# A row maximum that skips NaNs: keys on two engines against in-place halves on three, with longer loads and results stored by groups

## The chip, the cores and the metric

The kernel runs on one core of a Trainium2 chip. The metric is device time in microseconds for one execution, so lower is better. The core has several engines that run side by side: VectorE (DVE), ScalarE (ACT), GpSimd (POOL) and SyncE (SP), which here issues the transfers; 16 DMA engines move the data between the device's memory and the on-chip buffers of 128 partitions.

## The reference

The input is 32 x 2048 rows of 2048 float32 numbers, 512 MB in all, of which one in ten is NaN. For each row the largest number that is not NaN is wanted.

```python
def setup_inputs():
    batch, seq, dim = 32, 2048, 2048
    x = np.random.randn(batch, seq, dim).astype(np.float32)
    mask = np.random.rand(batch, seq, dim) < 0.1
    x[mask] = np.nan
    return {"x": x, "axis": -1}

def reference(x: np.ndarray, axis: int) -> np.ndarray:
    return np.nanmax(x, axis=axis).astype(np.float32)
```

Both kernels work on the bit patterns: they map them such that a NaN never wins.

## The kernel before

The 65536 rows are cut into 128 blocks. In a block each of the 128 partitions holds four whole rows, which lie next to each other in memory: 32 KB per partition, 4 MB per block, and the whole block is one contiguous piece of the input. The loop over the blocks `m` has three steps:

- SP issues the load of block `m` into `xt` (line 51, `xt<-in_x_dram`). The pool `io` has three buffers, and a buffer is free again once ACT has read it.
- ACT reads the numbers as int32 and writes a float32 key `kt` (line 53): the square of the scaled distance of the bit pattern from a constant. For numbers of the size drawn here the largest has the smallest key, and NaN a larger one. The pool `keys` has two buffers of 32 KB.
- DVE takes the minimum of the keys of each row (line 60, `acc<-kt`), four results per partition and block.

Behind the loop the 512 results per partition are turned back into numbers at once: a square root on ACT (line 70, with a table load of its own), two Newton rounds on DVE (lines 73 to 79), a linear step on ACT (line 81) and a cast (line 89). Then 64 transposes of 32x32 on DVE (line 100) bring them into the order of the output, and a single store writes them (line 104). The tile framework places the waits between the engines; each engine works through its instructions in program order.

Of the kernel before, what the change touches and what calls it, by code (L numbers as in the profile page):

```python
# [1 line left out]

# [4 lines left out]


@with_exitstack  # L10
def kernel(
    ctx: ExitStack,
    tc: tile.TileContext,
    x: bass.AP,
    axis: bass.AP,
    out: bass.AP,
):
    nc = tc.nc
    P = nc.NUM_PARTITIONS
    f32 = mybir.dt.float32  # L20
    i32 = mybir.dt.int32

    nd = len(x.shape)
    assert axis in (-1, nd - 1), axis
    D = x.shape[-1]

    x_bits = x.bitcast(i32).flatten_outer_dims()
    R = x_bits.shape[0]
    C = 4
    assert R % (P * C) == 0  # L30
    M = R // (P * C)
    x_ck = x_bits.rearrange("(m p c) d -> m p c d", p=P, c=C)

    out_flat = out.flatten_outer_dims().rearrange("r c -> (r c)")
    out_pn = out_flat.rearrange("(q s) -> q s", q=P)

    CG = float(0x50000000)
    SCALE = 2.0**-31
    BIAS = -CG * SCALE

    io = ctx.enter_context(tc.tile_pool(name="io", bufs=3))
    keys = ctx.enter_context(tc.tile_pool(name="keys", bufs=2))
    sing = ctx.enter_context(tc.tile_pool(name="sing", bufs=1))

    bias_t = sing.tile([P, 1], f32)
    nc.vector.memset(bias_t, BIAS)  # L46
    acc = sing.tile([P, M, C], f32)

    for m in range(M):
        xt = io.tile([P, C, D], i32)  # L50
        nc.sync.dma_start(out=xt, in_=x_ck[m])  # L51
        kt = keys.tile([P, C, D], f32)
        nc.scalar.activation(  # L53
            out=kt,
            in_=xt,
            func=mybir.ActivationFunctionType.Square,
            bias=bias_t,
            scale=SCALE,
        )
        nc.vector.tensor_reduce(  # L60
            out=acc[:, m, :],
            in_=kt,
            axis=mybir.AxisListType.X,
            op=mybir.AluOpType.min,
        )

    NQ = M * C
    accf = acc.rearrange("p m c -> p (m c)")
    y = sing.tile([P, NQ], f32)
    nc.scalar.activation(y, accf, mybir.ActivationFunctionType.Sqrt)  # L70
    for it in range(2):
        r = sing.tile([P, NQ], f32, tag=f"nr{it}")
        nc.vector.reciprocal(r, y)  # L73
        t = sing.tile([P, NQ], f32, tag=f"nt{it}")
        nc.vector.tensor_mul(t, accf, r)  # L75
        s = sing.tile([P, NQ], f32, tag=f"ns{it}")
        nc.vector.tensor_add(s, t, y)  # L77
        y = sing.tile([P, NQ], f32, tag=f"ny{it}")
        nc.vector.tensor_scalar_mul(y, s, 0.5)  # L79
    gf = sing.tile([P, NQ], f32)  # L80
    nc.scalar.activation(  # L81
        gf,
        y,
        mybir.ActivationFunctionType.Copy,
        bias=CG,
        scale=-(2.0**31),
    )
    gb = sing.tile([P, NQ], i32)
    nc.vector.tensor_copy(out=gb, in_=gf)  # L89

    B = 32
    assert M % P == 0
    U = M // P
    fin = sing.tile([P, U, P, C], i32)
    g4 = gb.rearrange("p (q u c) -> p q u c", u=U, c=C)
    for u in range(U):
        for j in range(C):
            for bi in range(P // B):
                for bj in range(P // B):
                    nc.vector.transpose(  # L100
                        out=fin[bi * B : (bi + 1) * B, u, bj * B : (bj + 1) * B, j],
                        in_=g4[bj * B : (bj + 1) * B, bi * B : (bi + 1) * B, u, j],
                    )
    nc.sync.dma_start(
        out=out_pn, in_=fin.rearrange("q u p c -> q (u p c)").bitcast(f32)
    )


# [1 line left out]
_INS = ['x', 'axis']  # L110
_OUTS = [((32, 2048), 'float32')]
#: Inputs that are plain numbers.
_NUMBERS = {'axis': -1}


# [26 lines left out]
```

## Time and profile before

| what | value |
|---|---|
| median of 12 runs | 1297.43 us (1297.26 to 1297.86) |
| profiled execution | 1297.38 us, span 1295.6 us |
| DVE, ACT, POOL busy | 1138.4, 915.4, 0.2 us |
| loads | 128 of 4096 KB, median 21.9 us from issue to landing |
| data moved | 537.19 MB, mean 415 GB/s over the span |

The span runs from the first to the last instruction. In a group's row stand its line, engine, operation, output and input with their shapes, the count, then the busy time in microseconds and the mean duration in nanoseconds, and last the idle time of the engine just before these instructions with what ended it. A timeline row begins with start and length in microseconds.

### The profile page before, as it was taken

Reading aid. Unit: us, or ns where it says so; the run is one execution under the profiler, and the core shown is the slowest. Engines: PE = TensorE matmul, PEld = TensorE weight load, DVE = VectorE, ACT = ScalarE, POOL = GpSimd, SP = SyncE. Lnnn points to the kernel's source line nnn. Section 1 sums busy time; section 2 is a strip of 40 time slices with the busy share of each in tenths; the row PEclk is TensorE's granted clock in tenths of the full one; section 3 lists DMA queues with packets and bytes.
Section 4 is the critical chain, followed back from the end, with each engine's and each line's share of the span. In section 5 each row is a group of like instructions: output and inputs, shape, how many; then the busy total and the mean of one; then the engine's idle time right before and its main releaser. Section 6 shows DMA issues by size and latency. Waiting matters only on the chain.

```text
span 1295.6 us, 761 instructions
## 1 busy us (share of the span) xinstructions
DVE 1138.4 (88%) x202; ACT 915.4 (71%) x132; POOL 0.2 (0%) x4
## 2 busy tenths in 40 slices
DVE  3988988988998988998998998998898998998998
ACT  4776776776776776776776776776777777777760
POOL 0000000000000000000000000000000000000000
DMA  9999999999999999999999999999999999999940
GB/s 405 437 430 428 437 432 426 437 434 424 436 435 425 434 435 425 435 435 425 435 435 425 436 434 427 434 434 429 431 436 427 431 437 428 430 437 428 430 197 8
DMA packets 18582, 537.19 MB, mean 415 GB/s; under 512 B 2064, under 2 KB 2064, under 8 KB 2192
## 3 DMA queue, kind: packets, MB, share of 16 engines
q1 hardware_dynamic: 18576, 537.14, 96.4%
q14 instruction: 6, 0.05, 0.0%
HBM read 536.87 MB, written 0.26 MB: 415 GB/s over the span
## 4 chain that ended last, share of the span: by engine, by line
DMA 73%; ACT 24%; DVE 3%; issue 0%; ACTq 0%; SPq 0%; DVEq 0%
DMA xt<-in_x_dram 73%; ACT kt L53 24%; DVE fin L100 1%; DVE acc L60 1%; DVE r L73 1%; DVE s L77 0%; DVE t L75 0%; DVE y L79 0%; ACTq L53 0%; ACT gf L81 0%; ACT y L70 0%; DVE gb L89 0%; SPq L51 0%; DVEq L137 0%
## 5 line engine op out<-in xcount | busy, mean ns | idle before, releaser
L60 DVE TENSOR_REDUCE acc<-kt 128x4 f32<-128x8192 f32 x128 | 1111.7, 8686 | 151.0 <-ACT kt L53 151.0
L53 ACT ACTIVATE kt<-xt,bias_t 128x8192 f32<-128x8192 int32 x128 | 911.6, 7122 | 329.0 <-DMA xt<-in_x_dram 329.0
L100 DVE STREAM_TRANSPOSE fin<-gb 32x32 int32<-32x32 int32 x64 | 15.9, 248 | 0.9
L53 ACT ACT_TABLE_LOAD x1 | 1.3, 1283 | 13.0 <-DMA xt<-in_x_dram 13.0
L81 ACT ACTIVATE gf<-y 128x512 f32<-128x512 f32 x1 | 0.6, 629 | 10.6 <-DVE y L79 10.6
L73 DVE RECIPROCAL r<-y 128x512 f32<-128x512 f32 x2 | 6.7, 3353 | 0.7 <-ACT y L70 0.7
L70 ACT ACTIVATE y<-acc 128x512 f32<-128x512 f32 x1 | 0.6, 629 | 7.5 <-DVE acc L60 7.5
L75 DVE TENSOR_TENSOR t<-acc,r 128x512 f32<-128x512 f32 x2 | 1.4, 691 | 0.1
L77 DVE TENSOR_TENSOR s<-t,y 128x512 f32<-128x512 f32 x2 | 1.4, 691 | 0.1
L70 ACT ACT_TABLE_LOAD x1 | 1.3, 1283 | 0.0
L89 DVE CAST gb<-gf 128x512 int32<-128x512 f32 x1 | 0.4, 427 | 0.7 <-ACT gf L81 0.7
L79 DVE TENSOR_SCALAR y<-s 128x512 f32<-128x512 f32 x2 | 0.9, 426 | 0.1
L46 DVE MEMSET bias_t<- 128x1 f32 x1 | 0.1, 59 | 0.8 <-PEq L123 0.8
L123 POOL MEMSET const-bfloat16-1.0<- 128x1 bf16 x1 | 0.1, 102 | 0.0
L123 POOL MEMSET const-uint8-127<- 128x1 uint8 x1 | 0.1, 102 | 0.0
L123 POOL MEMSET const-float32-0.0<- 128x1 f32 x1 | 0.1, 99 | 0.2 <-issue 0.2
L123 POOL MEMSET const-float32-1.0<- 128x1 f32 x1 | 0.1, 99 | 0.0
## 6 DMA issues: line engine op xcount, KB each, us to landing
xt<-in_x_dram SPq DMA_DIRECT2D x128, 4096.0 KB, 21.9
out_dram<-fin SPq DMA_DIRECT2D x1, 256.0 KB, 2.0
```

The lines of the kernel that those rows point to most:

```text
L46: nc.vector.memset(bias_t, BIAS)
L53: nc.scalar.activation(out=kt, in_=xt, func=mybir.ActivationFunctionType.Square, bias=bias_t, scale=SCALE,)
L60: nc.vector.tensor_reduce(out=acc[:, m, :], in_=kt, axis=mybir.AxisListType.X, op=mybir.AluOpType.min,)
L70: nc.scalar.activation(y, accf, mybir.ActivationFunctionType.Sqrt)
L73: nc.vector.reciprocal(r, y)
L75: nc.vector.tensor_mul(t, accf, r)
L77: nc.vector.tensor_add(s, t, y)
L79: nc.vector.tensor_scalar_mul(y, s, 0.5)
L81: nc.scalar.activation(gf, y, mybir.ActivationFunctionType.Copy, bias=CG, scale=-(2.0**31),)
L89: nc.vector.tensor_copy(out=gb, in_=gf)
L100: nc.vector.transpose(out=fin[bi * B : (bi + 1) * B, u, bj * B : (bj + 1) * B, j], in_=g4[bj * B : (bj + 1) * B, bi * B : (bi + 1) * B, u, j],
L123: nc = _bacc.Bacc("TRN2", target_bir_lowering=False, num_devices=1)
```

## The change

The work is laid out anew.

- The input is read in 16 groups of rows (`GROUPS`: a list of groups, each a list of tiles, each a list of loads, each a list of pieces, counted in rows per partition). Twelve groups have five tiles of eight rows per partition, so 40 rows; the four last have one tile of eight rows each. In a group each partition holds rows that lie next to each other: the load of a full tile takes 64 KB per partition, and in the large groups the pieces of neighbouring partitions lie 320 KB apart. The tiles of the last three groups are loaded in smaller parts: 4+2+2 rows, 2+2+1+1+1+1 rows, and eight single rows.
- There is no key tile. ACT, POOL and DVE work in turn on the same `xt`, in pieces of 3, 3 and 2 rows. ACT (line 94) reads the upper 16 bits of each number as int16 (every second 16-bit element) and writes uint16 in place: a number's upper half h becomes 0x7F7F - h, and the NaN's, on the other slope of Prelu, becomes 32768. POOL (line 102) computes 0x7F7F minus that, in place, as int16: a number gets its old upper half back, a NaN becomes a large negative number. DVE (line 110) takes the maximum of each row over the whole float32 numbers.
- `io` still has three buffers, now of 64 KB per partition; a buffer is free once DVE has reduced its last piece.
- At the end of each group two small DVE instructions (lines 118 and 127) turn a row of nothing but NaNs into NaN, and the group's results are stored without a transpose. The store of a group is issued on SP behind a load of the second next group (line 91), the last two at the end (line 132).
- A one-element activation ahead of the loop (line 71) loads the activation table.

```diff
+FULL = [[3, 3, 2]]
+GROUPS = [[FULL] * 5] * 12 + [
+    [FULL],
+    [[[2, 2], [2], [2]]],
+    [[[2], [2], [1], [1], [1], [1]]],
+    [[[1], [1], [1], [1], [1], [1], [1], [1]]],
+]
...
     io = ctx.enter_context(tc.tile_pool(name="io", bufs=3))
-    keys = ctx.enter_context(tc.tile_pool(name="keys", bufs=2))
+    res = ctx.enter_context(tc.tile_pool(name="res", bufs=3))
...
-    for m in range(M):
-        xt = io.tile([P, C, D], i32)
-        nc.sync.dma_start(out=xt, in_=x_ck[m])
-        kt = keys.tile([P, C, D], f32)
-        nc.scalar.activation(
-            out=kt,
-            in_=xt,
-            func=mybir.ActivationFunctionType.Square,
-            bias=bias_t,
-            scale=SCALE,
-        )
-        nc.vector.tensor_reduce(
-            out=acc[:, m, :],
-            in_=kt,
-            axis=mybir.AxisListType.X,
-            op=mybir.AluOpType.min,
-        )
...
+    stores = []
+    r0 = 0
+    for s, g in zip(rows, GROUPS):
+        xg = xr[r0 : r0 + P * s].rearrange("(p s) d -> p (s d)", p=P)
+        og = of[r0 : r0 + P * s].rearrange("(p s) -> p s", p=P)
+        r0 += P * s
+        acc = res.tile([P, s], f32, tag="acc")
+        at = 0
+        for tl in g:
+            xt = io.tile([P, WIDE * D], i32, tag="xt")
+            base = at
+            for ld in tl:
+                c = sum(ld)
+                nc.sync.dma_start(
+                    out=xt[:, (at - base) * D : (at - base + c) * D],
+                    in_=xg[:, at * D : (at + c) * D],
+                )
+                if len(stores) > 1:
+                    nc.sync.dma_start(**stores.pop(0))
+                for c in ld:
+                    xp = xt[:, (at - base) * D : (at - base + c) * D]
+                    nc.scalar.activation(
+                        out=xp.bitcast(u16)[:, 1::2],
+                        in_=xp.bitcast(i16)[:, 1::2],
+                        func=PRELU,
+                        bias=top,
+                        scale=-1.0,
+                        alpha=float(TOP - LOW) / (EDGE - NAN),
+                    )
+                    nc.gpsimd.tensor_scalar(
+                        out=xp.bitcast(i16)[:, 1::2],
+                        in0=xp.bitcast(u16)[:, 1::2],
+                        scalar1=-1.0,
+                        scalar2=float(TOP),
+                        op0=ALU.mult,
+                        op1=ALU.add,
+                    )
+                    nc.vector.tensor_reduce(
+                        out=acc[:, at : at + c],
+                        in_=xp.bitcast(f32).rearrange("p (c d) -> p c d", c=c),
+                        axis=mybir.AxisListType.X,
+                        op=ALU.max,
+                    )
+                    at += c
+        none = res.tile([P, s], i32, tag="none")
+        nc.vector.tensor_scalar(
+            out=none,
+            in0=acc,
+            scalar1=NONE,
+            scalar2=float(0x00C00000),
+            op0=ALU.is_equal,
+            op1=ALU.mult,
+        )
+        fin = res.tile([P, s], i32, tag="fin")
+        nc.vector.tensor_tensor(
+            out=fin, in0=acc.bitcast(i32), in1=none, op=ALU.bitwise_or
+        )
+        stores.append(dict(out=og, in_=fin))
+    for st in stores:
+        nc.sync.dma_start(**st)
```

Everything behind the old loop (lines 67 to 106 of the kernel before: root, Newton rounds, casts, transposes, the single store) is removed.

## Prediction

> **What bounds the kernel now.** I read four views. First the shares by engine and the chain that ended last:
>
> ```profile
> DVE 1138.4 (88%) x202; ACT 915.4 (71%) x132; POOL 0.2 (0%) x4
> DMA 73%; ACT 24%; DVE 3%; issue 0%; ACTq 0%; SPq 0%; DVEq 0%
> ```
>
> No compute engine is full, and the chain is DMA with ACT links. A chain "DMA 21.9, ACT 7.1, DMA 21.9" could mean a loop that waits for buffers, so the second view is the busy time by stretches (columns: stretch, length, DVE, ACT, POOL busy, clock, DMA share, GB/s):
>
> ```profile
> 100.00:600.00 500.00, 446.80 (x52) 366.62 (x52) 0.00 (x0) 1.00 1.00 432
> 600.00:1200.00 600.00, 535.97 (x63) 438.97 (x63) 0.00 (x0) 1.00 1.00 432
> 1247.00:1296.00 49.00, 42.16 (x75) 9.66 (x4) 0.00 (x0) 1.00 0.02 6
> ```
>
> The DMA share is 1.00 for the whole streaming part: the rings never run dry, so the transfer rate is the bound and the ACT links of the chain are only buffers handed back in time. The last stretch has no loads: 49 us of pure tail. Third, the timeline gives the ends of the stream and the order of the tail:
>
> ```profile
> 12.99 1.28 ACT L53 ACT_TABLE_LOAD   x1 [12.99 <-DMA xt<-in_x_dram]
> 21.44 17.28 DVE L60 TENSOR_REDUCE acc<-kt 128x4 f32<-128x8192 f32 x2 [20.58 <-ACT kt L53]
> ...
> 1247.71 7.12 ACT L53 ACTIVATE kt<-xt,bias_t 128x8192 f32<-128x8192 int32 x1 [2.58 <-DMA xt<-in_x_dram]
> 1254.85 1.28 ACT L70 ACT_TABLE_LOAD   x1
> 1254.87 8.69 DVE L60 TENSOR_REDUCE acc<-kt 128x4 f32<-128x8192 f32 x1 [1.01 <-ACT kt L53]
> 1263.59 0.63 ACT L70 ACTIVATE y<-acc 128x512 f32<-128x512 f32 x1 [7.45 <-DVE acc L60]
> ...
> 1275.97 16.72 DVE L100 STREAM_TRANSPOSE fin<-gb 32x32 int32<-32x32 int32 x64
> 1292.72 0.35 SPq L104 DMA_DIRECT2D out_dram<-fin  x1
> ```
>
> The first 4 MB land at 12.99 and the last at about 1247.7: 127 loads in 1234.7, so 9.72 us per load, 2.43 us per row of each partition. After the last landing come ACT 7.1, DVE 8.7, then 12.4 of root and Newton steps and cast (1263.6 to 1276.0), 16.7 of transposes, and 2.9 from the last transpose to the span's end: 48 in all. Last, the groups give the prices:
>
> ```profile
> L60 DVE TENSOR_REDUCE acc<-kt 128x4 f32<-128x8192 f32 x128 | 1111.7, 8686 | 151.0 <-ACT kt L53 151.0
> L53 ACT ACTIVATE kt<-xt,bias_t 128x8192 f32<-128x8192 int32 x128 | 911.6, 7122 | 329.0 <-DMA xt<-in_x_dram 329.0
> L75 DVE TENSOR_TENSOR t<-acc,r 128x512 f32<-128x512 f32 x2 | 1.4, 691 | 0.1
> L70 ACT ACTIVATE y<-acc 128x512 f32<-128x512 f32 x1 | 0.6, 629 | 7.5 <-DVE acc L60 7.5
> ```
>
> Two sizes of one engine give fixed part and slope. ACT: (7122-629)/7680 = 0.845 ns an element, 196 ns fixed. DVE: (8686-691)/7680 = 1.041 ns; two back-to-back reduces take 17.28, so 8.64 each, 0.11 us fixed.
>
> **The change part by part.**
>
> *The removed tail.* The root, both Newton rounds, the casts, the 64 transposes and the second table load go: 1263.6 to 1292.7, 29.1 us, all on the end path. All of it is gained only if nothing later takes its place.
>
> *The loads.* 61 of 8 MB, then 8 rows as 4+2+2, 8 as 2+2+1+1+1+1, 8 single rows. Bytes are the same, so 128 x 9.72 remains the floor: landing of tile 60 (the last full one) at 12.99-9.72+61x19.44 = 1189.1, of the last row 58.3 later, 1247.4. Two unknowns. Half as many long transfers may save something: the profile's best slices move 437 GB/s against a mean of 432, so 0 to 14 us if the whole gap were per-load cost; 2 is my value, as the rate is nearly flat. And a partition's run now lies 320 KB from the next one (40 rows of 8 KB) where it lay 32 KB. Here a rule of the Trainium skill speaks against the change ("DMA: Bandwidth & Descriptors", "Latency and other measured facts"): for 16 KB pieces, a row pitch of 512 KB gave 207 GB/s where the padded layout gave 214, and wider powers of two much less. The row here is 432 at a 32 KB pitch. Taken whole, 3.4% of 1234 is 42 us more; by the row, nothing. 320 KB is not a power of two and the pieces are 64 KB, so I take nothing, and keep 42 as an end.
>
> *Stores.* One store at the end becomes 16, on the SP queue with the loads. Each of the twelve 20 KB ones goes behind a load of two groups later, when its result is long done, so SP doesn't wait there. The old store took 2.0 from issue to landing; what one takes from the loads' engines lies between 0 and 0.5; 0.2 x 12 = 2.4. In the taper SP does wait: the store of tile 59's group blocks the loads behind it until tile 59 is reduced, that of tile 60 likewise, that of tile 61 likewise. About 9 us of load gaps follow, which the DVE backlog below covers. Without that cover they would be in the end.
>
> *Buffers.* kt goes; three xt of 64 KB are freed by DVE, not ACT. Per piece of 3, 3, 2 rows: ACT 0.196+0.845n = 5.39, 5.39, 3.66, sum 14.4; DVE 0.11+1.041n = 6.51, 6.51, 4.37, sum 17.39; both under the 19.44 of the transfer. With POOL as below, DVE starts a tile 11.0 after its landing and ends it at 28.4. The DMA has 38.9 of queued loads at that moment, so 10 us of slack for the next load: no gap.
>
> *POOL.* Before, POOL does four one-element memsets (102 ns); no row bounds its rate per element. Two statements of the Trainium skill, "GPSIMD Engine Reference", disagree: "Elementwise — side-by-side cycle accounting" has 1.03 cycles for bodies of up to two operations but calls 1.8 the best case of a tight loop, and "Performance pitfalls for Q7 kernels" gives about 1.9 for reads with small steps; "Engine selection" calls one-input work roughly line-rate. At its 1.2 GHz that is an estimate of 0.86 ns or of 1.5 to 1.6 ns. Per tile, with 0.2 fixed per instruction (twice the memset): 14.7 us or 25.2 us, against 19.44. By the first, POOL is hidden; by the second it is the bound. I take 0.86: the instruction has one tensor input, two operations and a 4-byte step[...]. The ends stay 0.85 and 1.6. The built program puts one set-up instruction ahead of POOL's first piece and ACT's table load ahead of the loop (1.28 in the old row); the first 8 MB land at 22.7, and the first buffer may come back 10 us late, so both are free up to that.
>
> *Group ends.* Two small DVE instructions per group, 16 times. By the rows 59 ns (memset) to 248 ns (transpose), 0.1 each, and 12 of the groups end in steady state where DVE has 2.05 idle a tile. The unknown is a lock with POOL: the Trainium skill ("SBUF — State Buffer", "Who interferes with whom") says a DVE operation with two SBUF inputs, or in a two-port mode, waits for a POOL instruction under way, while a reduce never does. No row here has both. Price 0 to 9 us on the four last groups (one POOL piece of up to 3.7 each for three of them); I take 1. In steady state up to 10 per group is covered by DVE's idle time (5 x 2.05).
>
> *The new tail.* At 1189.1 the last full tile lands, and DVE is still on the tile before. It starts tile 60 at 1200.1 and then has 17.39, tile 61 as four pieces of two rows (4 x 4.37 = 17.48), tile 62 (2 x 4.37 + 4 x 2.24 = 17.70) and tile 63 (8 x 2.24 = 17.92): 70.5, without a pause, since a row arrives each 2.43 and takes DVE 2.2. The taper lets DVE make up only some 10% of its lag. The reduces end at 1270.6, although the last row has landed by about 1257 with SP's gaps and passed ACT and POOL by 1261 (1.93 + 1.96). The store's 2.9 follows: 1273.5. Plus stores 2.4, lock 1, small operations 0.6, less 2 for the longer loads: a span of 1275.5. The profiled execution took 1297.38 for a span of 1295.6, so 1.8 lies around it: 1277.3, and as that execution is within 0.05 of the median of the twelve runs, it needs no other correction: 1277, a gain of 20. Of the 29 removed, about 9 come back as DVE's backlog: 48 us after the last landing become about 27.
>
> **The rivals.**
>
> *POOL becomes the bound (slower).* It decides from 1.15 ns an element: (19.44-0.6)/16384. At 1.5 ns a tile takes 25.2, 64 take 1611, and with start and end some 1645; at 1.6 about 1740. For it: two of the four statements, and 16-bit halves converted on both sides. Against it: one input, two operations. Chance 0.17.
>
> *The wide pitch slows the loads.* 42 us more on the DMA: it ends at about 1290, DVE catches up a little more, and the time is 1315. At half that price it would be about 1297, no change. Chance 0.08, of it 0.03 no change and 0.01 faster.
>
> *DVE isn't late.* If the taper did what its shape suggests, the end would be 1247.4 + 1.93 + 1.96 + 2.24 + 2.9 = 1256.4, time 1258, a little more with SP's gaps. DVE's 11 us start lag and 2.2 of 2.43 speak against it; a faster load rate doesn't help DVE. Chance 0.05.
>
> That the change isn't what it says is out: the built program has 61 long loads, three pieces per tile on each of three engines, and stores where the code has them.
>
> **How the numbers follow.** A measurement of this kernel tells about 0.2% (2.6 us) from no change. The forecast has 0.70, own range 1263 to 1292 (longer loads helping by up to 14, the lock by 9, stores by 6). With POOL 0.17, pitch 0.08, DVE in time 0.05: faster 0.70+0.05+0.01 = 0.76, same 0.03, slower 0.17+0.04 = 0.21. The range leaves out POOL's case and the best of the others: 1259 to 1316.
>
> **What would show it.** Right: POOL's groups at about 5.5 us for 128x6144; DMA share 1.00 to about 1190; the chain's last 70 us in the reduces of DVE without idle; the last load landing 10 us or more before the last reduce starts. Wrong: POOL busy over 95% with DVE waiting for it and the DMA share near 0.75 (the POOL rival); GB/s below 425 with all engines waiting for loads (pitch); DVE waiting for POOL in the last 20 us (DVE in time); idle before the two small DVE operations of several us (lock).

## The result and the profile after

The changed kernel takes 1284.56 us (median; 1284.3 to 1284.92) against 1297.42 before: a ratio of 0.9901, 95% interval 0.9892 to 0.991, so 12.9 us or 1.0% faster. The profiled execution has a span of 1282.7. The forecast was 1277, range 1259 to 1316.

The page of the changed kernel: busy time by engine, the chain that ended last, and the groups (busy, mean ns, idle before).

```profile
DVE 1143.1 (89%) x234; ACT 1203.8 (94%) x203; POOL 1204.4 (94%) x205
DMA 42%; POOL 23%; DVE 18%; ACT 12%; issue 5%; ACTq 0%; DVEq 0%
L110 DVE TENSOR_REDUCE acc<-xt 128x3 f32<-128x6144 f32 (+2 forms) x201 | 1116.0, 5582 | 135.4 <-POOL xt L102 135.4
L118 DVE TENSOR_SCALAR none<-acc 128x40 int32<-128x40 f32 (+1 forms) x16 | 24.7, 1543 | 0.4
```

ACT rose from 71% to 94% and POOL from nothing to 94%: two engines that the forecast had at three quarters are almost full. And sixteen small DVE operations (L118) take 1.5 us each on average instead of 0.1. The same groups with the shapes kept apart give the prices for the pieces:

```profile
L94 ACT ACTIVATE xt<-xt,top 128x6144 uint16<-128x6144 int16 x122 | 858.6, 7111 | 58.1 <-DMA xt<-in_x_dram 58.1
L102 POOL TENSOR_SCALAR xt<-xt 128x6144 int16<-128x6144 uint16 x122 | 856.7, 7022 | 60.5 <-ACT xt L94 55.7
L94 ACT ACTIVATE xt<-xt,top 128x2048 uint16<-128x2048 int16 x12 | 30.0, 2569 | 8.9 <-DMA xt<-in_x_dram 8.9
L102 POOL TENSOR_SCALAR xt<-xt 128x2048 int16<-128x2048 uint16 x12 | 29.6, 2465 | 3.8 <-ACT xt L94 2.9
```

From two sizes: ACT (7111-2569)/4096 = 1.109 ns an element, POOL (7022-2465)/4096 = 1.113. The loads still set the steady part (columns of the stretches as before):

```profile
100.00:600.00 500.00, 456.51 (x89) 483.90 (x78) 483.93 (x79) 1.00 1.00 432
600.00:1180.00 580.00, 530.63 (x102) 561.54 (x90) 562.73 (x90) 1.00 1.00 434
1180.00:1240.00 60.00, 58.27 (x15) 55.27 (x13) 58.74 (x12) 1.00 0.67 277
1240.00:1283.00 43.00, 40.16 (x20) 26.71 (x11) 30.53 (x13) 1.00 0.56 227
```

The DMA share is 1.00 up to 1180 and then falls to 0.67 and 0.56, while DVE is busy 98 of the last 103 us. The timeline shows this end (start, length, engine):

```profile
1185.86 46.81 ACT L94 ACTIVATE xt<-xt,top 128x6144 uint16<-128x6144 int16 x9 [0.65 <-DMA xt<-in_x_dram]
...
1200.24 6.55 DVE L110 TENSOR_REDUCE acc<-xt 128x3 f32<-128x6144 f32 x1
...
1222.33 4.09 DVE L118 TENSOR_SCALAR none<-acc 128x8 int32<-128x8 f32 x1
1226.27 4.41 DVE L110 TENSOR_REDUCE acc<-xt 128x2 f32<-128x4096 f32 x1
1230.60 0.62 DVE L127 TENSOR_TENSOR fin<-acc,none 128x8 int32<-128x8 int32 x1
...
1244.13 1.96 DVE L118 TENSOR_SCALAR none<-acc 128x8 int32<-128x8 f32 x1
...
1256.54 14.99 ACT L94 ACTIVATE xt<-xt,top 128x2048 uint16<-128x2048 int16 x6 [4.82 <-DMA xt<-in_x_dram]
...
1262.02 2.18 DVE L118 TENSOR_SCALAR none<-acc 128x8 int32<-128x8 f32 x1
...
1266.59 13.24 DVE L110 TENSOR_REDUCE acc<-xt 128x1 f32<-128x2048 f32 x6
1279.86 0.17 DVE L118 TENSOR_SCALAR none<-acc 128x8 int32<-128x8 f32 x1
```

Tile 60 has landed at 1185.86. DVE begins it at 1200.24 and then runs to 1279.86 with 0.4 us of idle time. In that run stand the three small pairs of groups 12 to 14 (counted from 0; a pair is L118 and L127): 4.09+0.62, 1.96+0.86 and 2.18+0.42, 10.1 us in all. The last pair, when POOL is done, takes 0.17+0.17.

### The profile page after: what moved, and what is told of

It reads as the page before. It is cut to its first block, busy times and chain, and to the rows that moved or that the text cites. A ratio compares the mean times of both kernels' runs of the same rounds, so it can differ in the third digit from the quotient of the medians.

```text
span 1282.7 us, 1065 instructions
## 1 busy us (share of the span) xinstructions
DVE 1143.1 (89%) x234; ACT 1203.8 (94%) x203; POOL 1204.4 (94%) x205
## 4 chain that ended last, share of the span: by engine, by line
DMA 42%; POOL 23%; DVE 18%; ACT 12%; issue 5%; ACTq 0%; DVEq 0%
DMA xt<-in_x_dram 42%; POOL xt L102 23%; DVE acc L110 18%; ACT xt L94 12%; DVE none L118 1%; DVE fin L127 0%; ACTq L94 0%; DVEq L110 0%; DVEq L127 0%
## 5 line engine op out<-in xcount | busy, mean ns | idle before, releaser
L102 POOL TENSOR_SCALAR xt<-xt 128x6144 int16<-128x6144 uint16 (+2 forms) x201 | 1204.2, 5991 | 69.7 <-ACT xt L94 58.6
L94 ACT ACTIVATE xt<-xt,top 128x6144 uint16<-128x6144 int16 (+2 forms) x201 | 1202.3, 6084 | 67.0 <-DMA xt<-in_x_dram 67.0
L110 DVE TENSOR_REDUCE acc<-xt 128x3 f32<-128x6144 f32 (+2 forms) x201 | 1116.0, 5582 | 135.4 <-POOL xt L102 135.4
L118 DVE TENSOR_SCALAR none<-acc 128x40 int32<-128x40 f32 (+1 forms) x16 | 24.7, 1543 | 0.4
L127 DVE TENSOR_TENSOR fin<-acc,none 128x40 int32<-128x40 int32 (+1 forms) x16 | 4.5, 280 | 0.4
```

What stands on the lines that cost most here:

```text
L94: nc.scalar.activation(out=xp.bitcast(u16)[:, 1::2], in_=xp.bitcast(i16)[:, 1::2], func=PRELU, bias=top, scale=-1.0, alpha=float(TOP - LOW ...
L102: nc.gpsimd.tensor_scalar(out=xp.bitcast(i16)[:, 1::2], in0=xp.bitcast(u16)[:, 1::2], scalar1=-1.0, scalar2=float(TOP), op0=ALU.mult, op1= ...
L110: nc.vector.tensor_reduce(out=acc[:, at : at + c], in_=xp.bitcast(f32).rearrange("p (c d) -> p c d", c=c), axis=mybir.AxisListType.X, op=A ...
L118: nc.vector.tensor_scalar(out=none, in0=acc, scalar1=NONE, scalar2=float(0x00C00000), op0=ALU.is_equal, op1=ALU.mult,)
L127: nc.vector.tensor_tensor(out=fin, in0=acc.bitcast(i32), in1=none, op=ALU.bitwise_or)
```

## The experiments

Two things had to be told apart: what the small pairs and the loads that SP holds back are worth at the end, and why ACT and POOL take 1.11 ns an element. The first theory was that the end is DVE's backlog (the work that lies before it and keeps it busy without a pause), in which the pairs wait for POOL ("lock"). The rival was that SP, waiting 65 us in all ahead of three stores, brings the last loads too late.

**Stores at the end.** The stores of the last five groups come behind all loads, and `res` gets six buffers instead of three to hold their results; nothing else changes.

```diff
-    res = ctx.enter_context(tc.tile_pool(name="res", bufs=3))
+    res = ctx.enter_context(tc.tile_pool(name="res", bufs=6))
...
-                if len(stores) > 1:
+                if len(stores) > 1 and gi < 13:
```

> The small DVE operations stay where they are; only the stores of the last five groups are issued after all loads, so that SP isn't held ahead of the late loads. Theory 'lock' with DVE's backlog as the end: the loads land some 10 us sooner and ACT and GpSimd finish sooner, but DVE has no idle time to give back: within 1.5 us of the changed kernel's 1284.56. It may move by the few us that a lock gets longer or shorter, since GpSimd's pieces then lie differently. Theory 'held loads': 9 to 10 us faster, 1275.

Measured: 1284.33 (1284.14 to 1284.55), 0.99 of before (0.9887 to 0.9913). The timeline has ACT and the last reduces:

```profile
1185.91 75.76 ACT L94 ACTIVATE xt<-xt,top 128x6144 uint16<-128x6144 int16 x21 [0.66 <-DMA xt<-in_x_dram]
...
1266.33 13.24 DVE L110 TENSOR_REDUCE acc<-xt 128x1 f32<-128x2048 f32 x6
```

ACT now works without a pause to 1261.7, so the loads are no longer late, and yet DVE's last reduces begin at 1266.33, where they began at 1266.59. The held loads cost nothing in the changed kernel; the rival is out.

**Small pairs deferred.** The last four groups share one result tile, and one pair over 32 columns comes behind all reduces (`finish` issues a pair and notes its stores); the stores of the last five groups are late, as above.

```diff
...
+        if gi < 12:
+            finish(acc, s, [og])
+        else:
+            touts.append(og)
...
+    finish(tacc, 32, touts)
```

> The two small DVE operations of the last four groups are moved behind all reduces (one pair over 32 columns instead of four pairs), and the stores of these groups and of the group before them go to the end, so that SP never waits ahead of a load. Theory 'lock': in the changed kernel these pairs took 10.1 us of DVE's time in its unbroken run from 1200.2 to 1280.2 because they wait for GpSimd instructions under way; taken away, DVE ends about 9 us sooner, less about 1 for four stores in a row: 1284.56 - 8 = 1276 to 1277. Theory 'held loads' (SP waits of 65 us ahead of the late loads set the end): also faster, by the about 10 us that ACT waited for the last two sets of loads (4.1 + 4.8), 1275; so this run alone doesn't tell them apart, stores_end does. If both are wrong: no change.

Measured: 1280.24 (0.9869, 0.9856 to 0.9882): 4.3 faster than the changed kernel, where 8 were expected. The direction holds, half of the gain doesn't. The timeline of this run says where most of it went:

```profile
1186.14 75.91 ACT L117 ACTIVATE xt<-xt,top 128x6144 uint16<-128x6144 int16 x21 [0.55 <-DMA xt<-in_x_dram]
1193.35 78.68 POOL L125 TENSOR_SCALAR xt<-xt 128x6144 int16<-128x6144 uint16 x21 [0.36 <-ACT xt L117]
1269.52 2.29 DVE L133 TENSOR_REDUCE tacc<-xt 128x1 f32<-128x2048 f32 x1 [0.25 <-POOL xt L125]
1272.06 2.29 DVE L133 TENSOR_REDUCE tacc<-xt 128x1 f32<-128x2048 f32 x1 [0.25 <-POOL xt L125]
```

DVE now waits 0.25 for POOL before each row, and ACT and POOL have 21 pieces without a pause. Behind DVE's backlog stood that of POOL: DVE's reduces end at 1274.34, only 5.5 earlier than in the changed kernel (1279.83). Of these, 1.4 are lost behind them, where four stores wait for the one pair, not one (from the last reduce to the end of the span 4.3 us, before 2.9). Note also the distance of the last two rows, 2.54 us: in pieces of one row POOL is slower than the loads (2.43 a row), so the finest part of the taper adds to its lag.

**The intermediate in PSUM.** One edit to the changed kernel takes away what the pair needs from the buffer's ports, with nothing moved (PSUM is a second on-chip memory, beside the buffer that holds the tiles):

```diff
+    ps = ctx.enter_context(
+        tc.tile_pool(name="ps", bufs=2, space=bass.MemoryType.PSUM)
+    )
...
-        none = res.tile([P, s], i32, tag="none")
+        none = ps.tile([P, s], i32, tag="none")
```

> The changed kernel with the intermediate of the small pair in PSUM instead of the on-chip buffer, nothing moved. Theory 'lock needs both sides in the buffer': the first of the pair falls from 1.4 (12 groups) and 2.7 (three tail groups) to about 0.2, the second, now with one input from the buffer, to 0.2; DVE's backlog is 9 shorter, and ACT and GpSimd become the end as in defer_small, with SP's held loads on top: 1280 to 1283. Rival 'any small DVE operation waits for GpSimd': the rows stay at 1 to 4 us and the time at 1284.5.

Measured: 1278.43 (0.9855, 0.9838 to 0.9871), 6.1 faster than the changed kernel and 1.6 below the range expected. The groups of the changed kernel (L118, L127) and of this run (L121, L130):

```profile
L118 DVE TENSOR_SCALAR none<-acc 128x8 int32<-128x8 f32 x4 | 8.4, 2100 | 0.0
L127 DVE TENSOR_TENSOR fin<-acc,none 128x8 int32<-128x8 int32 x4 | 2.1, 519 | 0.0
...
L121 DVE TENSOR_SCALAR none<-acc 128x40 int32<-128x40 f32 x12 | 2.4, 203 | 0.4
L121 DVE TENSOR_SCALAR none<-acc 128x8 int32<-128x8 f32 x4 | 0.6, 161 | 0.0
L130 DVE TENSOR_TENSOR fin<-acc,none 128x8 int32<-128x8 int32 x4 | 0.6, 154 | 0.0
```

The first of the pair fell from 2100 ns (8 columns) to 161, the second from 519 to 154. That is the lock shown: the same operation on the same data, beside the same POOL work, waits with its output in the buffer and doesn't with its output in PSUM. It is the rule that the forecast named (the Trainium skill, "SBUF — State Buffer", "Who interferes with whom"): an operation in a two-port mode, or with two inputs from the buffer, waits for POOL's instruction under way. The second of the pair has two such inputs; that the first is in a two-port mode is not shown by itself. The size is what it could not say: up to 4.1 us a time, with POOL pieces of 2.5 to 4.7. Here too DVE waits 0.25 for POOL before each of the last rows, and its reduces end at 1273.72; with one store behind the last pair instead of four, the span is 2.0 shorter than in the run before.

**Forms by themselves.** Two tiles of 2 MB, one instruction at a time, executed once.

> Not the task's computation: two 2 MB tiles, on which ACT, GpSimd and DVE run the changed kernel's instructions one at a time over 4096 elements, in forms that differ in the step of input and output and in the type; then twelve GpSimd instructions in a row beside which DVE runs reduces and the small pair, once with the intermediate in the on-chip buffer and once in PSUM. In the changed kernel ACT took 4845 ns and GpSimd 4746 for 4096 elements (1.11 ns an element), ACT in the kernel before 0.845 an element, so 3660. Theory 'step': writing (or reading) 16-bit values at a step of 4 bytes costs a third more, alone too: 4.8 us for the stepped form, 3.7 for the contiguous one, and the two mixed forms tell reading from writing. Theory 'contention': ACT and GpSimd slow each other in the kernel; alone the stepped form takes 3.7. Theory 'type': all 16-bit forms take 4.8. Lock: with GpSimd busy the small DVE operation with an output in the buffer takes 1 to 4 us, the reduces their usual 4.4; if a lock needs both sides in the buffer, the PSUM versions take about 0.2.

The timeline (lines 87 and 89 to 92 are ACT: stepped to stepped in place; stepped to contiguous; contiguous to stepped; contiguous to contiguous; int32 to float32. Lines 97, 99 and 102 are POOL: stepped to stepped, stepped to contiguous, int32 to float32. "Stepped" is every second 16-bit value):

```profile
9.84 4.82 ACT L87 ACTIVATE t<-t,top 128x4096 uint16<-128x4096 int16 x1
19.55 3.71 ACT L89 ACTIVATE t<-t,top 128x4096 uint16<-128x4096 int16 x1
23.29 4.84 ACT L90 ACTIVATE t<-t,top 128x4096 uint16<-128x4096 int16 x1
28.16 3.71 ACT L91 ACTIVATE t<-t,top 128x4096 uint16<-128x4096 int16 x1
31.90 3.71 ACT L92 ACTIVATE t<-t,top 128x4096 f32<-128x4096 int32 x1
...
49.14 4.72 POOL L97 TENSOR_SCALAR t<-t 128x4096 int16<-128x4096 uint16 x1 [48.70 <-ACTq L178]
58.73 3.60 POOL L99 TENSOR_SCALAR t<-t 128x4096 int16<-128x4096 uint16 x1
70.92 3.60 POOL L102 TENSOR_SCALAR t<-t 128x4096 f32<-128x4096 int32 x1
...
98.92 0.62 DVE L134 TENSOR_SCALAR s<-sm 128x8 int32<-128x8 f32 x1
```

Alone, with no other engine at work, ACT takes 4.82 for the stepped form, as much as in the kernel (4845 ns): no contention. It is the stepped write of 16-bit values: 4.8 whenever the output is stepped, 3.7 whenever it isn't, whatever the input's step and type (an int32 input with the stepped output, line 94, takes 4.82 too). POOL does the same, 4.7 against 3.6. So 0.27 ns an element comes with the step of the 16-bit output; why, no run shows. The small pair beside a busy POOL took 0.62 here (line 134), ending about where POOL's first two instructions of 4.8 us do (89.99 + 9.6): the reduces of 4.4 had used up most of the wait. The PSUM forms fell just behind that point, so this run alone didn't show whether they escape the lock; the run before did.

**No taper.** Full tiles to the end.

```diff
-    [[[2, 2], [2], [2]]],
-    [[[2], [2], [1], [1], [1], [1]]],
-    [[[1], [1], [1], [1], [1], [1], [1], [1]]],
+    [FULL],
+    [FULL],
+    [FULL],
```

> The last three groups have full tiles of one 8 MB load and pieces of 3, 3, 2 rows, like the rest. Theory: the taper doesn't shorten the end, as DVE (and ACT and GpSimd) are a tile behind anyway: the last tile lands at about 1185.9 + 3 x 19.4 = 1244, its first piece comes to DVE 14.1 later, 17.4 of reduces, small pair and store 2.9: 1278.5 and 1.8 around: 1280, faster than with the taper by 4, since the locks of three groups fall into DVE's idle time instead of its backlog. Rival 'the taper does its work': without it the last tile's 14.1 + 17.4 come on top of a longer lag, 1290 and more.

Measured: 1281.11 (0.9875, 0.986 to 0.989). The timeline around the pair of group 12:

```profile
1218.42 1.42 DVE L118 TENSOR_SCALAR none<-acc 128x8 int32<-128x8 f32 x1
...
1226.95 10.88 DVE L110 TENSOR_REDUCE acc<-xt 128x3 f32<-128x6144 f32 x2 [0.43 <-POOL xt L102]
```

The changed kernel with its taper is 3.4 us slower. In this run the first operations of the pairs of groups 12 to 14 take 1.42, 1.55 and 1.57, where DVE would wait for POOL anyway; with the taper they lie in its unbroken run. So what costs is the pairs that the taper exposes, not the taper: with the intermediate in PSUM the tapered kernel is 2.7 faster than this one (1278.43). No run has PSUM and no taper together.

**Whole pieces.** FULL = [[8]], each engine takes the 64 KB of a partition at once.

> A full tile is one piece of 8 rows for each engine. By the measured slopes ACT takes 18.5, GpSimd 18.3 and DVE 17.2 for it, each below the load's 19.39, but one after the other: the buffer comes free 54 us after the landing, and with three buffers a tile then takes (54 + 2.5 + 19.4)/3 = 25.3 us: 64 x 25.3 = 1620 us. If latency didn't matter (each engine below the load's time): about 1300, with 20 us more of tail.

Measured: 1662.32 (1.2813, 1.2787 to 1.2838). All three engines are below the load's 19.39 for a tile (18.4, 18.3, 17.2 by this run), and still:

```profile
ACT xt L94 <- DMA xt<-in_x_dram: 452.9, 63, 20.6
POOL xt L102 <- ACT xt L94: 463.5, 61, 40.9
...
1185.50 15.45 DVE L118 TENSOR_SCALAR none<-acc 128x40 int32<-128x40 f32 x1
```

Each engine waits 450 us, for the engine ahead of it, and ACT for loads that wait for a buffer. A tile takes 25.37 us on average (ACT's first pieces of tiles 0 and 60 begin at 22.85 and 1545.13), as the sum of the expectation has it; that sum left out the first landing and the end. It is a tile's load and its way through three engines, shared among three buffers, that decides here; with three buffers, the pieces of 3, 3, 2 rows are what makes the long loads possible. The last line shows the lock once more: beside POOL pieces of 18.3 the first of a pair takes up to 15.45.

**Split loads, and split loads with deferred pairs.** FULL = [[3], [3], [2]]: three DMAs per tile, so ACT can begin after three rows.

> One edit to the changed kernel: a full tile is loaded by three DMAs of 3, 3 and 2 rows, so ACT can begin after 3 rows instead of 8. Theory 'tile lag': in the taper ACT is a whole tile behind (it gets tile 60 at 1185.9 and then works 75.8 us without a pause on 32 rows, at 2.37 a row against 2.43 of the loads, so it never catches up). With the lag cut to 3 rows, ACT, GpSimd and DVE all end soon after the last landing: landing of the last row about 1247 plus gaps from SP's waits ahead of the stores (up to 10, no longer covered), 7.3 for one row through three engines, 2.9 for the store, 1.8 around: 1259 to 1269. Rival 'rate': smaller loads cost so much (more packets, more issues) that a tile takes over 19.5 us: slower than 1284.56 by 0.1 x 61 and more. Rival 'lock alone': DVE's locks set the end whatever the loads do: 1280 to 1284.

> Split loads and the deferred small operations and late stores together. Theory 'tile lag': neither the lag nor the locks nor SP's waits are left in the taper: 1247 + 7.3 + 2.9 + 1.8 = 1259, with ACT's 2.50 a row against 2.43 in the single-row part (12 rows x 0.07) 1260. If the lag were not it, 1280 as in defer_small.

Measured: 1280.12 (0.9867, 0.9852 to 0.9881) and 1278.52 (0.9853, 0.9837 to 0.987). Both expectations were missed, by 11 us (from the upper end of the range) and by 19. Lines of split_defer (start, length) and a stretch of it show why:

```profile
10.36 7.08 ACT L117 ACTIVATE xt<-xt,top 128x6144 uint16<-128x6144 int16 x1 [8.13 <-DMA xt<-in_x_dram]
...
1184.29 7.09 ACT L117 ACTIVATE xt<-xt,top 128x6144 uint16<-128x6144 int16 x1 [0.49 <-DMA xt<-in_x_dram]
...
1206.26 57.13 ACT L117 ACTIVATE xt<-xt,top 128x4096 uint16<-128x4096 int16 x18 [2.90 <-DMA xt<-in_x_dram]
1211.17 59.36 POOL L125 TENSOR_SCALAR xt<-xt 128x4096 int16<-128x4096 uint16 x18 [0.61 <-ACT xt L117]
...
600.00:1180.00 580.00, 527.03 (x102) 560.32 (x90) 554.37 (x90) 1.00 1.00 430
```

The rate fell from 434 (changed kernel, same stretch) to 430 GB/s. ACT's first pieces of tiles 0 and 60 begin at 10.36 and 1184.29, 19.57 a tile, where the changed kernel has 22.55 and 1185.86, 19.39: 10.6 us over the 60 tiles. And the taper begins with a load of four rows: ACT waits for it until 1206.26 and from then on works without a pause, 2.38 a row against 2.43 of the loads. As I read it, an engine that needs 98% of the loads' time keeps as its lag the largest load it last had to wait for.

**Late split.** The groups chosen by that reading: 40 full tiles, 21 in three loads, then loads of two rows; the last 72 rows are one group with one pair and one store.

```diff
...
+PART = [[3], [3], [2]]
+TWOS = [[2], [2], [2], [2]]
+GROUPS = (
+    [[FULL] * 5] * 8
+    + [[PART] * 5] * 3
+    + [[PART] * 6 + [TWOS, TWOS, [[2], [2], [2], [1], [1]]]]
+)
```

> Only the list of groups is edited: 40 full tiles as in the changed kernel, then 21 tiles loaded as 3, 3 and 2 rows, then three tiles of loads of two rows with two single rows at the very end; the last 72 rows are one group, so that no small pair and no held store lies in the last 170 us. Theory 'rate': ACT works at 18.9 to 19.1 us a tile against 19.4 to 19.5 of the loads, so it keeps as its lag the largest load it last had to wait for, and needs about 18 tiles to work a lag of 8 rows down to one of 3; split_defer kept 9.7 us of lag because its taper begins with a load of four rows, and it paid 0.11 us a tile for the small loads. Here: last landing 3.1 + 40 x 19.39 + 21 x 19.50 + 24 x 2.43 = 1246.5; ACT ends about 5 later, GpSimd 2.5, DVE 2.3, small pair and stores 3: span 1260, time 1261 to 1266. Rival 'the engines' own rate is the end': ACT and GpSimd need 2.38 a row whatever the loads are, and never get rid of the 8 rows: 1278.

Measured: 1271.33 (1270.93 to 1271.68; 0.9799, 0.9784 to 0.9814): the fastest version, 13.2 below the changed kernel and 26 below the one before, but 5 above the upper end of what was expected. Its end:

```profile
1177.16 76.62 ACT L95 ACTIVATE xt<-xt,top 128x6144 uint16<-128x6144 int16 x16 [0.47 <-DMA xt<-in_x_dram]
1257.21 8.81 DVE L111 TENSOR_REDUCE acc<-xt 128x2 f32<-128x4096 f32 x3 [0.38 <-POOL xt L103]
...
1242.84 19.41 POOL L103 TENSOR_SCALAR xt<-xt 128x4096 int16<-128x4096 uint16 x5
POOL xt L103 <- ACT xt L95: 46.9, 40, 29.2
```

ACT ends at 1253.8, but POOL's last piece only at 1262.25 (1242.84 + 19.41). POOL has a lag of its own behind ACT. The last line says that it waited for ACT 40 times; the last of these waits ends at 785.85, at the last of the 40 tiles loaded in one piece. From there it works through 200 rows without a wait, 476.4 us or 2.38 a row: POOL's own rate sets this end. The expectation had counted one row of lag there.

What the run shows of the reading is therefore mixed. Against defer_small, which loads full tiles in one piece to the end, ACT starts tile 60 at 1177.16 instead of 1186.14, 9.0 earlier, and the time is 8.9 shorter, about 1 of it by fewer stores at the end: here the smaller lag pays. Against split_defer it is 7.2 shorter, but its tile 60 also comes 7.1 earlier (1177.16 against 1184.29), and that is the loads' rate: 40 tiles at 19.39 instead of 19.57. ACT's smaller lag in the taper brings nothing more at the end, because POOL stands behind it.

**The pitch.** Groups of 8 and of 16 tiles put neighbouring partitions' runs 512 and 1024 KB apart. The page's rule in the two expectations is that of the forecast's pitch rival (the Trainium skill, "DMA: Bandwidth & Descriptors", "Latency and other measured facts").

> Groups of eight tiles instead of five, so that the 64 KB runs of neighbouring partitions lie 512 KB apart instead of 320 KB. Forecast of the page's rule on row pitch (207 of 214 GB/s): a tile each 19.39 x 1.034 = 20.05 us in the steady part, 60 x 0.66 = 40 us more, less DVE's smaller backlog: about 1318. Forecast of the prediction's choice (pitch doesn't matter at 64 KB runs): 19.39 us a tile, within 2 us of 1284.56; five group ends fewer lie in covered time.

> Groups of sixteen tiles: runs of neighbouring partitions 1024 KB apart in 48 of 64 tiles, 832 KB in thirteen. The 512 KB pitch gave runs from 1285.1 to 1298.8 where 320 KB gave 1284.3 to 1284.9, so the pitch costs something in some runs. If the page's rule holds in kind for 64 KB runs, 1 MB is worse than 512 KB, between 3% and 25% on the loads: 1315 or more. If the spread of the 512 KB runs has another cause, about 1285, or the same spread.

Measured: at 512 KB 1294.1, with twelve runs spread over 1285.06 to 1298.81 (ratio 0.998, 0.9966 to 0.9993); at 1024 KB 1328.17 (1.0238, 1.0207 to 1.0269). The stretch 100 to 600 has 421 GB/s at 1024 KB against 432 at 320 KB:

```profile
100.00:600.00 500.00, 444.78 (x78) 471.11 (x77) 471.61 (x76) 1.00 1.00 421
...
25.83 18.68 ACT L93 ACTIVATE xt<-xt,top 128x6144 uint16<-128x6144 int16 x3 [23.61 <-DMA xt<-in_x_dram]
...
357.81 7.03 DVE L126 TENSOR_TENSOR fin<-acc,none 128x128 int32<-128x128 int32 x1
```

At 1024 KB the loads themselves are slower from the start: the first tile lands at 25.83 instead of 22.55 and the second comes 22.69 later instead of 19.32, before any group has ended, so the groups' size isn't the reason there. Later the two mix: the first tiles of the second and third group come late too, but there stands the pair of the group before, whose second operation, now over 128 columns, takes 7.03 (0.20 over 40). How much of the 43.6 us is the pitch alone, no run separates. The only profile at 512 KB is of its fastest execution and shows the full rate, so what slows the others stays open.

## Why the prediction was right, and where not

- **The direction and the mechanism held.** The loads stay the bound in the steady part, the old tail of 29.1 us goes, and part of it comes back as a DVE run without pause from tile 60 to the last row. DVE was forecast to start tile 60 at 1200.1 and started at 1200.24. stores_end shows that SP's held loads lie under this backlog, as was said (about 9 us of gaps forecast, 4.08 + 4.82 in ACT's waits), and no_taper that the taper, with the pairs in it, doesn't shorten the end. DVE's price, worked out from two different operations, came out too: 6.51 us forecast for three rows, 6.55 measured.
- **The start time was right by two errors.** The landing of tile 60 came at 1185.9, not 1189.1 plus 2.4 for stores less 2: a tile takes 19.39, stores included; most take 19.35, the ones with a store 0.05 more, not 0.2. And DVE's lag was 14.4, not 11.0, because ACT took 7.1 and POOL 7.0 for the first piece, not 5.4 and 5.5. That the two nearly cancel is luck.
- **The term that was too small: the lock**, "Price 0 to 9 us on the four last groups ...; I take 1". The small operations took 10.1 us in the last run of DVE, where 1.6 had been put down for lock and operations together. These 8.5 are more than the whole error of the span (1282.7 against 1275.5). The bound was right, the choice within it was not: beside an engine that is 94% busy, the first of a pair waited every time but the last (1.2 to 1.5 us in the twelve large groups, 2.0 to 4.1 in three small ones; 0.17 in the last, when POOL was done). The sign named for it, idle time before the two operations, didn't show (0.0 to 0.4 us in all): the wait stands in the operation's own duration.
- **The price per element on ACT and POOL** was too low: ACT's came from a row with a 32-bit result (0.845), POOL's from the page named there (0.86). With stepped 16-bit results it is 1.11, as the forms show. The sign "POOL's groups at about 5.5 us" came out at 7.0, and where the last row was to have passed ACT and POOL by 1261, POOL ended at 1274.33. In the changed kernel this adds 3.4 to DVE's lag (above); it also set what comes next (defer_small stops after 4.3 of 8.5).
- **The POOL rival was close.** Its point of decision was 1.15 ns an element, POOL has 1.113. POOL took 1204 us where some 940 were forecast (64 tiles of 14.7). Of the four statements of the Trainium skill, "GPSIMD Engine Reference", that the forecast set side by side, the one for bodies of up to two operations ("Elementwise — side-by-side cycle accounting": 1.03 cycles, an estimate of 0.86 ns) agrees with the contiguous form, 3.60 us for 4096 elements or 0.88 ns each; 1.8 or 1.9 cycles as a floor do not. None of the figures is that of the stepped form.
- **The pitch rival**: nothing to be seen at 320 KB (434 GB/s in the changed kernel's second half against 432 before), as was chosen; at 1024 KB a cost is there.
- **DVE in time** didn't happen: DVE ran to the end with 0.4 us of idle time.

## What to carry to other kernels

When a bound engine's tail is replaced by finer work, ask of each engine how far behind it is when the last large load lands and how much faster than the loads it works: at 98% of the loads' time a taper gives back little (2.38 us a row against 2.43), and in pieces of one row nothing (2.54). A tiny VectorE operation beside a busy GpSimd can cost almost as much as the GpSimd instruction that it meets (4.1 of 4.7 us, 15.45 of 18.3); an intermediate in PSUM, or putting the operation where VectorE waits anyway, takes that away. Price an instruction from a row with the same output type and step, not only the same engine and size.

## What was not expected of the hardware

- The step of a 16-bit output, not that of the input, costs ACT and POOL nearly a third: 4.82 against 3.71 and 4.72 against 3.60 us for 4096 elements. A float32 result, which also advances 4 bytes an element, is not slower (ACT 3.71, POOL 3.60).
- Loads of 64 KB per partition move 432 to 434 GB/s, three loads of 24, 24 and 16 KB 430 (19.39 and 19.57 us for 8 MB).
- At a 512 KB pitch the time of one kernel spread over 14 us from run to run, at 1024 KB over 9, where the other versions stayed within 1.
